# The last row tiles of a decoder trunk by halves of the tokens, with the final products in another place of VectorE's queue

## The chip, the cores and the metric

The kernel runs on one core of one Trainium2 chip. Its time is the device time of one execution in microseconds (us); the median of three executions stands for it. A core has the engines TensorE (PE in the profile; PEld is its loading of weights), VectorE (DVE), ScalarE (ACT) and GpSimd (POOL), each with its own queue of instructions that it works through in order, a SyncE (SP) that issues transfers, and 16 DMA engines that carry them. ScalarE issues transfers too, from its own queue.

## The reference

A trunk of two layers over 512 tokens with 1024 features, in float32. Cut to what matters here:

```python
for i in range(DEPTH):                       # DEPTH = 2
    ...                                      # mixing of tokens, output projection, residual add
    u = jnp.einsum('bsd,df->bsf', rms_norm(x, norm_mlp[i]), w_up[i])
    x = x + jnp.einsum('bsf,fd->bsd', jnp.square(jax.nn.relu(u)), w_down[i])
    gate = jax.nn.sigmoid(jnp.einsum('bsd,de->bse', rms_norm(x, norm_ple[i]), w_ple_gate[i]))
    x = x + gate * jnp.einsum('bsk,kd->bsd', p[i], w_ple_proj[i])
return rms_norm(x, norm_final)               # x * rsqrt(mean(x*x) + eps) * gain
```

The change lies in the last two lines of the last layer: the gate's projection (1024 by 1024), the projection of the embedding `p` (256 by 1024), the residual add, and the final norm, whose sum runs over all 1024 features of a token.

## The kernel before, in words

Features lie on the partitions and tokens along the free dimension: the residual `X` is eight row tiles of 128 features by 512 tokens, `X[0]` to `X[7]`. A weight tile is 128 by 128; four of them are one transfer of 256 KB (`raw`), which ScalarE rounds to `whi` (line 175) and VectorE turns into the rest `wlo` (line 177). Every product of 128 by 128 by N is three matmuls (lines 218 to 220 in `mm3`: high by high, high by low, low by high), so a row tile of the gate is 8 products, 24 matmuls, into the PSUM tile `gate`, and the projection of `p` is 2 products, 6 matmuls, into the PSUM tile `ple`. A row tile m of the last stage so takes 30 matmuls on TensorE, and then the function `gated` on VectorE and ScalarE: `gu` is the gate times the norm of the layer (line 1156, VectorE, reads `gate`), a tanh (line 1157, ScalarE), `gu` times `ple` (line 1158, VectorE) and the add into `X[m]` (line 1159, VectorE). The square `sq` of `X[m]` follows on ScalarE, it is added to `acc`, and ScalarE scales `X[m]` by the gain `gf`.

In the last layer the row tiles 0 to HALF - 1 are made over all 512 tokens at once, the others twice, for the tokens 0 to 255 and then for 256 to 511, with the same weights. HALF is 5, so three row tiles go by halves. When the last row tile of a half is there, the norm of its tokens is closed: `ss` sums `acc` and the last square over the partitions (line 225, TensorE, small matmuls of one column each, their 64 output rows at a time), ten small instructions on VectorE make the inverse root `rT` (lines 1198 and 230 to 239), and `row_of` (line 266, TensorE, two transposes) spreads it as the row `rb` over all partitions in PSUM (`pr`). ScalarE copies `pr` to `Rs` in SBUF (line 1205). Then come the final products `fin`, X times that row, 128 by 256 each (line 1212), in groups of two row tiles, and each group goes out by a transfer of 256 KB (line 1213), in turn from ScalarE's and SyncE's queue. VectorE makes all eight products of the first half from `pr`, and six of the second; GpSimd makes the two of row tiles 6 and 7 of the second half from `Rs`.

The order of the instructions in an engine's queue is fixed before the run: a scheduler orders them by its own simulation of times and by priorities; the code inside `hp_(3000)` has a higher priority. A dependency added by `add_manual_dep` with the class NoSync orders two instructions of an engine and adds no semaphore. On the chip each instruction then waits in its queue for the semaphores that it names, and everything behind it waits with it.

Of the kernel before, what the change touches and what calls it, by code (L numbers as in the profile page):

```python
# [8 lines left out]
F32 = mybir.dt.float32  # L9
# [4 lines left out]
ALU = mybir.AluOpType  # L14
# [25 lines left out]
    ("pkq", 0, 3): 194, ("pov", 0, 0): 349, ("x1p", 0, 0): 385, ("pv", 0, 1): 460, ("pkq", 1, 0): 246,  # L40
    ("psq", 1, 11): 283,
}
HALF = 5
PEND = 4
PEND2 = 3
RB, HIB, LOB, USB = 3, 4, 6, 8
# [41 lines left out]
def trunk(ctx, tc, xT, xK, pT, posr, pos, wfm, wtm, consts, negi, smalls, gfin, out, dbg=None, depth=L):  # L88
# [9 lines left out]
    def mm_tile(name="mm"):  # L98
        return pp.tile([128, 512], F32, tag="mm", name=name, bufs=2)

    def ps_tile(shape, name):
        return pp.tile(shape, F32, tag="pg", name=name, bufs=2)

    def pa_tile(shape, name):
        return pp.tile(shape, F32, tag="pa", name=name, bufs=4)
# [46 lines left out]
    def hp_(n=HPRI):  # L152
        return tc.high_priority(offset=n)
# [43 lines left out]
    @contextmanager  # L197
    def grp(name, i=0):

        n0 = len(nc.cur_bb.bb.instructions)  # L200
        yield
        new = [q for q in nc.cur_bb.bb.instructions[n0:] if q.engine == mybir.EngineType.PE]
        if name == "large":
            large.setdefault(curl[0], []).extend(new)
        else:
            groups.setdefault((name, curl[0], i), []).extend(new)

    def queue_behind():
        for (name, l, i), n in ANCH.items():
# [185 lines left out]
    for l in range(depth):  # L395
# [758 lines left out]
        def gated(m, ts, ps, pq):  # L1154
            u = hp.tile([128, T], F32, tag="ha", name="gu", bufs=2)[:, ts]
            V.tensor_tensor(u, ps, R[:, ts], ALU.mult)
            A.activation(out=u, in_=u, func=ACTF.Tanh, scale=0.5)
            V.scalar_tensor_tensor(u, u, 1.0, pq, ALU.add, ALU.mult)
            V.scalar_tensor_tensor(X[m][:, ts], u, 0.5, X[m][:, ts], ALU.mult, ALU.add)
# [9 lines left out]
        if final:  # L1169

            for m in range(HALF):
                A.activation(out=X[m], in_=X[m], func=ACTF.Copy, scale=gf[:, m:m + 1])
            outs = []
            nw = 10
            w_t = [w_next() for _ in range(nw * (8 - HALF))]
            pq_t = None
            for hf in range(2):
                ts = slice(256 * hf, 256 * hf + 256)
                for m in range(HALF, 8):
                    w_m = w_t[nw * (m - HALF):nw * (m - HALF) + nw]  # L1180
                    ps = pa_tile([128, 256], "gate")
                    mm3(ps, [(h[:, ts], o[:, ts]) for h, o in XG], True, True, w_m[0:8])
                    pq = mm_tile("ple")[:, 0:256]
                    mm3(pq, [(h[:, ts], o[:, ts]) for h, o in pS], True, True, w_m[8:10])
                    gated(m, ts, ps, pq)
                    q = tp.tile([128, T], F32, tag="sq", name="sq", bufs=2)
                    A.activation(out=q[:, ts], in_=X[m][:, ts], func=ACTF.Square)
                    if m < 7:
                        V.tensor_tensor(nrm.acc[:, ts], nrm.acc[:, ts], q[:, ts], ALU.add)
                    A.activation(out=X[m][:, ts], in_=X[m][:, ts], func=ACTF.Copy, scale=gf[:, m:m + 1])  # L1190
                with hp_(3000):
                    ss = ps_tile([128, 2], "ss")
                    for b in range(2):
                        bs = slice(256 * hf + 128 * b, 256 * hf + 128 * b + 128)
                        mm_cols(ss[:, b:b + 1], nrm.acc[:, bs], ones[:, 0:1], True, False)
                        mm_cols(ss[:, b:b + 1], q[:, bs], ones[:, 0:1], False, True)
                    ms = pad(tp, [128, 2], "ms", "ms", 2)
                    V.tensor_scalar(ms, ss, 1.0 / D, EPS, ALU.mult, ALU.add)
                    rT = pad(tp, [128, 2], "rT", "rT", 2)
                    rsqrt(rT, ms, [128, 2], tp, "rn")  # L1200
                    pr = ps_tile([128, 256], "rb")
                    for b in range(2):
                        row_of(pr[:, b * 128:(b + 1) * 128], rT[:, b:b + 1])
                    Rs = hp.tile([128, 256], F32, tag="Rs", name="Rs", bufs=2)
                    A.activation(out=Rs, in_=pr, func=ACTF.Copy)
                outs.append((ts, pr, Rs))
            for ts, pr, Rs in outs:
                for g, ms_g in enumerate(((0, 1), (2, 3), (6, 7), (4, 5))):
                    o_t = hp.tile([128, 256 * len(ms_g)], F32, tag="fin", name="fin", bufs=8)
                    for j, m in enumerate(ms_g):  # L1210
                        e, r_ = (G, Rs) if (g == 2 and ts.start) else (V, pr)
                        e.tensor_tensor(o_t[:, 256 * j:256 * j + 256], X[m][:, ts], r_, ALU.mult)
                    (nc.sync if g % 2 else nc.scalar).dma_start(out=out[ms_g[0]:ms_g[-1] + 1, :, ts].rearrange("m p t -> p m t"),
                                      in_=o_t.rearrange("p (m t) -> p m t", t=256))
        mlp.close()
    queue_behind()

# [129 lines left out]
```

## Time and profile before

| | us |
|---|---|
| median of 3 runs | 1347.64 |
| lowest and highest | 1347.39, 1347.97 |
| profiled execution, its own time | 1348.9 |
| its span, first to last instruction | 1347.1 |
| TensorE busy in the span | 1308.8 |
| VectorE busy | 819.6 |
| ScalarE busy | 606.5 |

The profile is of one execution; the times in its views count from the start of the span. A row of the timeline gives start, duration, engine, line, operation, written tile <- read tiles, shapes, count, and in brackets how long the engine had been idle and which instruction released it. A row of the stretches gives the busy time of each engine in that stretch (with the count), TensorE's granted clock as a share of full speed, the share of the DMA engines and GB/s.

### The profile page before, as it was taken

How to read it: one execution, taken by the hardware profiler on the slowest of the kernel's cores; microseconds unless marked ns; L12 is line 12 of the kernel's file. 1: busy time of each engine (PE TensorE's matmuls, PEld its weight loads, DVE VectorE, ACT ScalarE, POOL GpSimd, SP SyncE). 2: the span in 40 equal slices, each digit the busy share in tenths (PEclk: the TensorE clock that was granted, in tenths of full speed). 3: DMA queues.
4: the chain of work that ended last, by engine and by line, in shares of the span. 5: the costliest groups of instructions: out<-in, count | busy, mean ns of one | idle time of the engine just before them, and what ended most of it. 6: DMA issues, size and time to landing. Idle time of an engine off the chain costs nothing.

```text
span 1347.1 us, 21029 instructions
## 1 busy us (share of the span) xinstructions
PE 1308.8 (97%) x7772; PEld 1081.6 (80%) x7772; DVE 819.6 (61%) x1765; ACT 606.5 (45%) x1245; POOL 133.6 (10%) x151
## 2 busy tenths in 40 slices
PE   9979999999999999999999999999999999999996
PEld 8757787888888888888887877778888888888886
DVE  5967989754443443455768789877534434344565
ACT  6464674543342432444446546635524324234452
POOL 1031330200000000010112223102000000000110
PEclk9969999999999999999999999999999999999998
DMA  7233231333333333333433322223333333333331
GB/s 251 87 98 86 58 111 56 111 93 101 96 97 99 94 96 100 95 101 104 130 109 102 108 68 79 76 74 106 96 94 96 100 94 101 95 95 101 94 103 63
DMA packets 89751, 131.94 MB, mean 98 GB/s; under 512 B 21664, under 2 KB 30368, under 8 KB 89648
## 3 DMA queue, kind: packets, MB, share of 16 engines
q1 hardware_dynamic: 88560, 129.55, 32.1%
q8 instruction: 61, 1.00, 0.3%
q10 hardware_dynamic: 1088, 1.05, 0.2%
q14 instruction: 42, 0.34, 0.1%
HBM read 125.02 MB, written 5.54 MB: 97 GB/s over the span
## 4 chain that ended last, share of the span: by engine, by line
PE 86%; DVE 9%; issue 1%; DMA 1%; ACT 1%; SPq 1%; DVEq 0%; ACTq 0%
PE up L218 9%; PE up L219 9%; PE down L219 9%; PE up L220 9%; PE down L218 9%; PE down L220 9%; PE proj L218 3%; PE proj L219 3%; PE proj L220 3%; PE outp L218 2%; PE gate L218 2%; PE gate L220 2%; PE gate L219 2%; PE outp L219 2%; PE outp L220 2%
## 5 line engine op out<-in xcount | busy, mean ns | idle before, releaser
L175 ACT ACTIVATE whi<-raw 128x512 fp32r<-128x512 f32 x404 | 253.5, 631 | 532.1 <-PE down L219 227.6
L177 DVE TENSOR_TENSOR wlo<-raw,whi 128x512 fp32r<-128x512 f32 x404 | 288.8, 718 | 166.2 <-ACT whi L175 165.1
L218 PE MATMUL down<-hidh,whi 128*128 128x512 f32 x512 | 199.3, 389 | 0.0
L218 PE MATMUL up<-xsh,whi 128*128 128x512 f32 x512 | 199.1, 390 | 0.0
L219 PE MATMUL up<-xsl,whi 128*128 128x512 f32 x512 | 199.0, 389 | 0.0
L220 PE MATMUL up<-xsh,wlo 128*128 128x512 f32 x512 | 199.0, 389 | 0.0
L220 PE MATMUL down<-hidh,wlo 128*128 128x512 f32 x512 | 198.0, 389 | 0.0
L219 PE MATMUL down<-hidl,whi 128*128 128x512 f32 x512 | 198.0, 389 | 0.0
L279 POOL TENSOR_TENSOR acc<-acc,sq 128x512 f32<-128x512 f32 x29 | 40.1, 1381 | 848.9 <-ACT sq L278 848.9
L218 PE MATMUL proj<-xsh,whi 128*128 128x512 f32 x304 | 122.4, 403 | 0.2
L219 PE MATMUL proj<-xsl,whi 128*128 128x512 f32 x304 | 121.3, 399 | 0.0
L220 PE MATMUL proj<-xsh,wlo 128*128 128x512 f32 x304 | 120.9, 398 | 0.0
L1133 DVE TENSOR_TENSOR X<-X,down 128x512 f32<-128x512 f32 x64 | 44.0, 687 | 115.0 <-PE down L220 115.0
L218 PEld LDWEIGHTS down<-hidh,whi 128*128 128x128 f32 x512 | 96.1, 188 | 20.1
L218 PEld LDWEIGHTS up<-xsh,whi 128*128 128x128 f32 x512 | 96.1, 188 | 19.9
L220 PEld LDWEIGHTS up<-xsh,wlo 128*128 128x128 f32 x512 | 96.1, 188 | 19.9
L219 PEld LDWEIGHTS down<-hidl,whi 128*128 128x128 f32 x512 | 96.1, 188 | 19.8
L220 PEld LDWEIGHTS down<-hidh,wlo 128*128 128x128 f32 x512 | 96.1, 188 | 19.9
L219 PEld LDWEIGHTS up<-xsl,whi 128*128 128x128 f32 x512 | 96.1, 188 | 19.8
L1124 DVE SCALAR_TENSOR_TENSOR ha<-up,R 128x512 f32<-128x512 f32 x64 | 44.0, 691 | 91.2 <-PE up L220 88.5
L246 DVE TENSOR_TENSOR hidl<-hf,hidh 128x512 fp32r<-128x512 f32 x64 | 44.3, 692 | 43.9 <-ACT hidh L245 43.9
L218 PEld LDWEIGHTS proj<-xsh,whi 128*128 128x128 f32 x304 | 58.1, 191 | 12.8 <-ACT sqq L581 0.4
(361 smaller groups left out, 2084.2 us busy)
## 6 DMA issues: line engine op xcount, KB each, us to landing
raw<-wfm SPq DMA_DIRECT2D x404, 256.0 KB, 2.6
X<-xT SPq DMA_DIRECT2D x16, 256.0 KB, 4.6
raw<-wtm SPq DMA_DIRECT2D x16, 200.0 KB, 3.9
xk<-xK SPq DMA_DIRECT2D x8, 256.0 KB, 4.6
gr<-scr SPq DMA_DIRECT2D x8, 256.0 KB, 4.1
Mr<-scr SPq DMA_DIRECT2D x8, 256.0 KB, 3.8
xd<-X SPq DMA_DIRECT2D x8, 256.0 KB, 2.3
X<-xd SPq DMA_DIRECT2D x8, 256.0 KB, 3.4
```

What stands on the lines that cost most here:

```text
L175: A.activation(out=hi, in_=raw, func=ACTF.Copy)
L177: (G if (i % NCH) * WC < WPOOL else V).tensor_tensor(lo, raw, f(hi), ALU.subtract)
L218: PE.matmul(out=ps, lhsT=wh, rhs=ah, start=start and k == 0, stop=False)
L219: PE.matmul(out=ps, lhsT=wh, rhs=al, start=False, stop=False)
L220: PE.matmul(out=ps, lhsT=wl, rhs=ah, start=False, stop=stop and k == n - 1)
L246: V.tensor_tensor(lo, src, f(hi), ALU.subtract)
L279: (G if self.n < 6 else V).tensor_tensor(self.acc, self.acc, q, ALU.add)
L1124: V.scalar_tensor_tensor(a_t, ps, 0.0, R, ALU.max, ALU.mult)
L1133: V.tensor_tensor(X[m], X[m], ps, ALU.add)
```

## The change: what it does

Four edits in the last stage, and bookkeeping around them.

1. HALF goes from 5 to 4: row tile 4 is now also made by halves. The stretches of tokens stand in PARTS, (256, 256) as before.
2. The function `last_on` finds the instruction that was last put into VectorE's queue. After each `gated` of a half it notes the add into `X[m]`. Each of the first half's final products is ordered on VectorE behind the noted instruction BEH = -3 of the second half, that is the add into `X[5]` for the tokens 256 to 511.
3. In the first half no `Rs` is made any more (no one read it there). In the second half the row is spread twice: `pr` as before, for VectorE, and `p2` in a PSUM tile of the kind that the gates use, which ScalarE copies to `Rs` for GpSimd.
4. The `fin` tiles are 768 wide and six instead of 512 wide and eight; small tiles of the norm have other names.

```diff
--- before.py
+++ after.py
@@ -40,7 +40,9 @@
     ("pkq", 0, 3): 194, ("pov", 0, 0): 349, ("x1p", 0, 0): 385, ("pv", 0, 1): 460, ("pkq", 1, 0): 246,
     ("psq", 1, 11): 283,
 }
-HALF = 5
+HALF = 4
+PARTS = (256, 256)
+BEH = -3
 PEND = 4
 PEND2 = 3
 RB, HIB, LOB, USB = 3, 4, 6, 8
@@ -204,6 +206,9 @@
             large.setdefault(curl[0], []).extend(new)
         else:
             groups.setdefault((name, curl[0], i), []).extend(new)
+
+    def last_on(engine):
+        return next(q for q in reversed(nc.cur_bb.bb.instructions) if q.engine == engine)
 
     def queue_behind():
         for (name, l, i), n in ANCH.items():
@@ -1173,45 +1178,58 @@
             outs = []
             nw = 10
             w_t = [w_next() for _ in range(nw * (8 - HALF))]
-            pq_t = None
-            for hf in range(2):
-                ts = slice(256 * hf, 256 * hf + 256)
+            t0 = 0
+            for n in PARTS:
+                ts = slice(t0, t0 + n)
+                t0 += n
+                done = []
                 for m in range(HALF, 8):
                     w_m = w_t[nw * (m - HALF):nw * (m - HALF) + nw]
-                    ps = pa_tile([128, 256], "gate")
+                    ps = pa_tile([128, n], "gate")
                     mm3(ps, [(h[:, ts], o[:, ts]) for h, o in XG], True, True, w_m[0:8])
-                    pq = mm_tile("ple")[:, 0:256]
+                    pq = mm_tile("ple")[:, 0:n]
                     mm3(pq, [(h[:, ts], o[:, ts]) for h, o in pS], True, True, w_m[8:10])
                     gated(m, ts, ps, pq)
+                    done.append(last_on(mybir.EngineType.DVE))
                     q = tp.tile([128, T], F32, tag="sq", name="sq", bufs=2)
                     A.activation(out=q[:, ts], in_=X[m][:, ts], func=ACTF.Square)
                     if m < 7:
                         V.tensor_tensor(nrm.acc[:, ts], nrm.acc[:, ts], q[:, ts], ALU.add)
                     A.activation(out=X[m][:, ts], in_=X[m][:, ts], func=ACTF.Copy, scale=gf[:, m:m + 1])
+                nb = n // 128
                 with hp_(3000):
-                    ss = ps_tile([128, 2], "ss")
-                    for b in range(2):
-                        bs = slice(256 * hf + 128 * b, 256 * hf + 128 * b + 128)
+                    ss = ps_tile([128, nb], "ss")
+                    for b in range(nb):
+                        bs = slice(ts.start + 128 * b, ts.start + 128 * b + 128)
                         mm_cols(ss[:, b:b + 1], nrm.acc[:, bs], ones[:, 0:1], True, False)
                         mm_cols(ss[:, b:b + 1], q[:, bs], ones[:, 0:1], False, True)
-                    ms = pad(tp, [128, 2], "ms", "ms", 2)
+                    ms = pad(tp, [128, nb], f"ms{n}", f"ms{n}", 2)
                     V.tensor_scalar(ms, ss, 1.0 / D, EPS, ALU.mult, ALU.add)
-                    rT = pad(tp, [128, 2], "rT", "rT", 2)
-                    rsqrt(rT, ms, [128, 2], tp, "rn")
-                    pr = ps_tile([128, 256], "rb")
-                    for b in range(2):
+                    rT = pad(tp, [128, nb], f"rT{n}", f"rT{n}", 2)
+                    rsqrt(rT, ms, [128, nb], tp, f"rn{n}")
+                    pr = ps_tile([128, n], "rb")
+                    for b in range(nb):
                         row_of(pr[:, b * 128:(b + 1) * 128], rT[:, b:b + 1])
-                    Rs = hp.tile([128, 256], F32, tag="Rs", name="Rs", bufs=2)
-                    A.activation(out=Rs, in_=pr, func=ACTF.Copy)
-                outs.append((ts, pr, Rs))
-            for ts, pr, Rs in outs:
+                    Rs = None
+                    if t0 == T:
+                        p2 = pa_tile([128, n], "rb")
+                        for b in range(nb):
+                            row_of(p2[:, b * 128:(b + 1) * 128], rT[:, b:b + 1])
+                        Rs = hp.tile([128, n], F32, tag="Rs", name="Rs")
+                        A.activation(out=Rs, in_=p2, func=ACTF.Copy)
+                outs.append((ts, n, pr, Rs, done))
+            for k, (ts, n, pr, Rs, _) in enumerate(outs):
                 for g, ms_g in enumerate(((0, 1), (2, 3), (6, 7), (4, 5))):
-                    o_t = hp.tile([128, 256 * len(ms_g)], F32, tag="fin", name="fin", bufs=8)
+                    o_t = hp.tile([128, 768], F32, tag="fin", name="fin", bufs=6)[:, 0:n * len(ms_g)]
                     for j, m in enumerate(ms_g):
-                        e, r_ = (G, Rs) if (g == 2 and ts.start) else (V, pr)
-                        e.tensor_tensor(o_t[:, 256 * j:256 * j + 256], X[m][:, ts], r_, ALU.mult)
+                        e, r_ = (G, Rs) if g == 2 and Rs is not None else (V, pr)
+                        e.tensor_tensor(o_t[:, n * j:n * j + n], X[m][:, ts], r_, ALU.mult)
+                        if Rs is None:
+
+                            tc.add_manual_dep(last_on(mybir.EngineType.DVE), outs[k + 1][4][BEH].name, mybir.DependencyInfo(
+                                mybir.DependencyClass.NoSync, mybir.DependencyReason.DATA), reason="order on VectorE")
                     (nc.sync if g % 2 else nc.scalar).dma_start(out=out[ms_g[0]:ms_g[-1] + 1, :, ts].rearrange("m p t -> p m t"),
-                                      in_=o_t.rearrange("p (m t) -> p m t", t=256))
+                                      in_=o_t.rearrange("p (m t) -> p m t", t=n))
         mlp.close()
     queue_behind()
```

Up to the last row tiles the queues of all engines are the same in both kernels, line numbers aside (a line of `mm3` is 5 higher after the change, and `fin` is L1226 in place of L1212). On VectorE the first half's final products stood in a row before the last row tile's `gu` times `ple`. Before:

```order
L239 SCALAR_TENSOR_TENSOR rT<-rnw,rT 128x2
L1158 SCALAR_TENSOR_TENSOR gu<-gu,ple 128x256
L1159 SCALAR_TENSOR_TENSOR X<-gu,X 128x256
L1189 TENSOR_TENSOR acc<-acc,sq 128x256
L1156 TENSOR_TENSOR gu<-gate,R 128x256
L1212 TENSOR_TENSOR fin<-X,rb 128x256 x8
L1158 SCALAR_TENSOR_TENSOR gu<-gu,ple 128x256
L1159 SCALAR_TENSOR_TENSOR X<-gu,X 128x256
L1198 TENSOR_SCALAR ms<-ss 128x2
L230 TENSOR_SCALAR rnw<-ms 128x2
```

Here `gu<-gate`, `gu<-ple` and `X<-gu,X` are the steps of `gated`, and `ms<-ss` opens the closing of the norm. With the change, in the same place of the queue (the end of the second half):

```order
L1163 SCALAR_TENSOR_TENSOR gu<-gu,ple 128x256
L1164 SCALAR_TENSOR_TENSOR X<-gu,X 128x256
L1197 TENSOR_TENSOR acc<-acc,sq 128x256
L1226 TENSOR_TENSOR fin<-X,rb 128x256 x5
L1161 TENSOR_TENSOR gu<-gate,R 128x256
L1226 TENSOR_TENSOR fin<-X,rb 128x256 x3
L1163 SCALAR_TENSOR_TENSOR gu<-gu,ple 128x256
L1164 SCALAR_TENSOR_TENSOR X<-gu,X 128x256
L1161 TENSOR_TENSOR gu<-gate,R 128x256
L1197 TENSOR_TENSOR acc<-acc,sq 128x256
L1163 SCALAR_TENSOR_TENSOR gu<-gu,ple 128x256
L1164 SCALAR_TENSOR_TENSOR X<-gu,X 128x256
```

The eight products are now around the `gu<-gate` of row tile 6, five ahead of it and three behind; the last row tile's three steps have only an add to `acc` between them.

What each first product of a half waits for is in the rows with their semaphores. Before, for the second half:

```order
L237 TENSOR_TENSOR rnw<-rT 128x2 [waits DVE_49]
L238 SCALAR_TENSOR_TENSOR rnw<-rnw,ms 128x2 [waits DVE_49]
L239 SCALAR_TENSOR_TENSOR rT<-rnw,rT 128x2 [waits DVE_49]
L1212 TENSOR_TENSOR fin<-X,rb 128x256 [waits Activation_49]
L1212 TENSOR_TENSOR fin<-X,rb 128x256 x5
```

and with the change:

```order
L243 SCALAR_TENSOR_TENSOR rn256w<-rn256w,ms_13238 128x2 [waits DVE_49]
L244 SCALAR_TENSOR_TENSOR rT_13240<-rn256w,rT_13240 128x2 [waits DVE_49]
L1226 TENSOR_TENSOR fin<-X,rb 128x256 [waits PE_49]
L1226 TENSOR_TENSOR fin<-X,rb 128x256 x3
L1226 TENSOR_TENSOR fin<-X,rb 128x256 [waits DMAHW4_49]
L1226 TENSOR_TENSOR fin<-X,rb 128x256
```

The first product waited for ScalarE (its copy of `pr`) and now waits for TensorE. The fifth waits for a transfer of the first half, whose `fin` tile it takes.

On TensorE the end of the queue was, before:

```order
L219 MATMUL ple<-pSl,whi 128x256
L220 MATMUL ple<-pSh,wlo 128x256
L225 MATMUL ss<-cst,acc 64x1 x2
L225 MATMUL ss<-cst,sq 64x1 x2
L225 MATMUL ss<-cst,acc 64x1 x2
L225 MATMUL ss<-cst,sq 64x1 x2
L266 MATMUL rb<-cst,rT 128x128 x2
```

and is now:

```order
L224 MATMUL ple<-pSl,whi 128x256
L225 MATMUL ple<-pSh,wlo 128x256
L230 MATMUL ss<-cst,acc 64x1 x2
L230 MATMUL ss<-cst,sq 64x1 x2
L230 MATMUL ss<-cst,acc 64x1 x2
L230 MATMUL ss<-cst,sq 64x1 x2
L271 MATMUL rb<-cst,rT_13240 128x128 x4
```

Behind the two transposes of `pr` stand the two of `p2`.

## Prediction

> **What bounds the kernel now.** I read the page first, then the chain of waits, the stretches and the timeline of the last 45 us, since the queues differ nowhere else.
>
> ```profile
> span 1347.1 us, 21029 instructions
> PE 86%; DVE 9%; issue 1%; DMA 1%; ACT 1%; SPq 1%; DVEq 0%; ACTq 0%
> ```
>
> The chain is TensorE's for most of the span. What this change can move is the piece behind TensorE's last product and the length of TensorE's own work ahead of it. The stretches below are the row tiles of the last stage: row tile 4 over all tokens, row tile 7 of the first half, and row tiles 5, 6 and 7 of the second half.
>
> ```profile
> 1303.51:1310.31 6.80, 6.80 (x32) 5.63 (x31) 5.40 (x9) 6.10 (x11) 2.60 (x2) 1.00 0.47 145
> ...
> 1317.50:1321.10 3.60, 3.60 (x33) 3.60 (x31) 1.69 (x4) 1.34 (x4) 0.00 (x0) 1.00 0.00 0
> 1321.10:1325.10 4.00, 4.00 (x37) 3.85 (x35) 1.27 (x3) 1.34 (x4) 0.00 (x0) 1.00 0.00 0
> 1325.10:1329.33 4.23, 4.23 (x44) 4.08 (x43) 2.88 (x13) 1.34 (x4) 0.00 (x0) 1.00 0.01 4
> 1329.33:1333.14 3.81, 3.81 (x34) 3.76 (x32) 1.95 (x6) 1.73 (x5) 0.00 (x0) 1.00 0.01 2
> ```
>
> TensorE has no idle time in any of them: up to 1333.14 its length sets the end. A half takes 3.60 where nothing is put in, and 4.00, 4.23 and 3.81 where the first half's `ss` and `rb` are. Behind it VectorE and ScalarE set the end:
>
> ```profile
> 1316.98 0.42 DVE L1156 TENSOR_TENSOR gu<-gate,R 128x256 f32<-128x256 f32 x1 [0.78 <-PE gate L220]
> 1318.86 0.42 ACT L1187 ACTIVATE sq<-X 128x256 f32<-128x256 f32 x1 [1.00 <-DVE X L1159]
> 1320.58 0.42 DVE L1156 TENSOR_TENSOR gu<-gate,R 128x256 f32<-128x256 f32 x1 [0.85 <-PE gate L220]
> ...
> 1332.62 0.42 DVE L1156 TENSOR_TENSOR gu<-gate,R 128x256 f32<-128x256 f32 x1 [1.05 <-PE gate L220]
> 1332.96 2.73 DVE L1212 TENSOR_TENSOR fin<-X,rb 128x256 f32<-128x256 f32 x8
> 1335.61 0.41 DVE L1158 SCALAR_TENSOR_TENSOR gu<-gu,ple 128x256 f32<-128x256 f32 x1
> 1336.51 0.42 ACT L1187 ACTIVATE sq<-X 128x256 f32<-128x256 f32 x1 [3.02 <-DVE X L1159]
> ```
>
> Row tile 6 of the first half shows `gated` undisturbed: 1.88 from `gu` to `sq`. The last row tile takes 3.89, because eight `fin` products of the first half, which nobody needs yet, stand in VectorE's queue ahead of its `gu` times `ple`. What follows is serial:
>
> ```profile
> 1336.98 0.38 PE L225 MATMUL ss<-cst,sq 128*64 128x1 f32 x4 [3.47 <-ACT sq L1187]
> ...
> 1337.43 0.36 PE L225 MATMUL ss<-cst,sq 128*64 128x1 f32 x4
> 1337.84 0.16 DVE L1198 TENSOR_SCALAR ms<-ss 128x2 f32<-128x2 f32 x1 [1.36 <-PE ss L225]
> 1339.92 0.66 PE L266 MATMUL rb<-cst,rT 128*128 128x128 f32 x2 [2.13 <-DVE rT L239]
> 1340.61 0.38 ACT L1205 ACTIVATE Rs<-rb 128x256 f32<-128x256 f32 x1 [3.14 <-PE rb L266]
> 1341.03 2.08 DVE L1212 TENSOR_TENSOR fin<-X,rb 128x256 f32<-128x256 f32 x6 [1.26 <-ACT Rs L1205]
> 1341.07 1.41 POOL L1212 TENSOR_TENSOR fin<-X,Rs 128x256 f32<-128x256 f32 x2 [26.92 <-ACT Rs L1205]
> 1341.81 1.13 ACTq L1213 DMA_DIRECT2D outT<-fin  x2
> ```
>
> VectorE's last products read `pr` in PSUM, yet wait for ScalarE's copy of it, 0.42 after the row was there.
>
> **The change part by part.**
>
> *Row tile 4 by halves.* It takes 2 x 3.60 = 7.20 in place of 6.80. The second half then has four row tiles, with `ss` and `rb` in the first three of them, so the last one is free of them. Its start on TensorE is 1303.51 + 4 x 3.60 + 4.00 + 4.23 + 3.81 = 1329.95, and its `gu` comes 3.08 later (1317.50 to 1320.58 in the first half): 1333.03, against 1332.62. Cost: +0.41.
>
> The Trainium skill ("TensorE: Matmul & The Clock Gate", Back-to-back issue gap) gives N / 2.4 + 2.5 ns between warm matmuls; an estimate by it is 30 x 216 = 6.47 for the whole row tile and 60 x 109 = 6.55 for two halves, a cost of 0.08 and a sum 0.3 lower. The trace disagrees: 3.60 / 30 is 120 ns for N = 256, with the loading of weights busy all the time, and 6.80 / 30 is 227 for N = 512.
>
> *The eight products out of the last row tile.* Undisturbed, its `sq` comes 1.88 after `gu`: 1333.03 + 1.88 = 1334.91. Before it took 3.89. Gain: -2.01. The products go to row tile 6 of the second half, whose `gu` can start at 1303.51 + 14.40 + 4.00 + 4.23 + (1332.62 - 1329.33) = 1329.43. They wait for the first half's `rb`, which stands 21 products into that row tile:
>
> ```profile
> 1325.67 0.28 PE L225 MATMUL ss<-cst,sq 128*64 128x1 f32 x4
> ...
> 1325.92 0.26 PE L225 MATMUL ss<-cst,sq 128*64 128x1 f32 x4
> ...
> 1331.85 0.38 PE L266 MATMUL rb<-cst,rT 128*128 128x128 f32 x2
> ...
> 1332.27 0.39 ACT L1205 ACTIVATE Rs<-rb 128x256 f32<-128x256 f32 x1 [0.61 <-PE rb L266]
> ```
>
> Before, the row could be read 0.35 ahead of that row tile's `gu` (1332.27 against 1332.62), so the products start at 1329.08. One takes 0.331 (1332.96 to 1335.61 for eight). Five end at 1330.74, `gu` of row tile 6 goes then, 1.31 late, the other three end at about 1332.07, and `gu` times `ple` and the add follow by about 1332.87. Behind them in the queue is the last row tile's `gu`, due at 1333.03: 0.16 of slack, so I cost the delay at nothing. The cover is TensorE's work on the last row tile; if each product took its whole 0.42 instead, that `gu` would be 8 x 0.09 - 0.16 = 0.55 late. Two transfers now stand in ScalarE's queue around row tile 6's tanh; the first is free with the second product, at about 1329.8, before that tanh is due at 1331.2, and the second behind it, before `sq`: nothing.
>
> *The row twice.* VectorE need not wait for ScalarE: it starts where `Rs` started before. Gain: 1341.03 - 1340.61 = 0.42, taken as -0.41 since its wait ends about 0.01 after the row. The price is on GpSimd's path: two more transposes stand ahead of `Rs`. The bounds for the pair are 0.2 (a warm pair of transposes lengthens a half by 3.81 - 3.60) and 0.66 (the cold row's whole duration). GpSimd ended its products 1.87 after `Rs` started (1342.48), so it would end 2.07 to 2.53 after VectorE's start, where VectorE's own six end at 2.08. Does the last transfer mind?
>
> ```profile
> DMA  0000000000000005999999999999999200000000
> GB/s 0 0 0 0 0 0 0 0 0 0 0 0 0 0 0 185 387 392 335 346 387 381 387 387 381 392 381 370 387 392 358 64 0 0 0 0 0 0 0 0
> ```
>
> These are 40 slices of 1340.00 to 1347.10, 0.1775 each. Once the second half's transfers run (from 1342.66, 0.85 after the first issue), the DMA engines are full until all four are through, 2.75 for 1.05 MB, 0.69 each. The third transfer's turn comes 0.78 + 0.85 + 2 x 0.69 = 3.0 after VectorE's first product; GpSimd's is ready 2.07 + 0.85 = 2.9 to 3.4 after it, and SyncE's last one, ready at 2.9, fills a hole. So the end follows VectorE's first product: cost 0, at most 0.25 if half the hole stays.
>
> *TensorE's clock behind its last product.*
>
> ```profile
> 1335.75:1336.00 0.25, 0.00 (x0) 0.00 (x0) 0.25 (x1) 0.00 (x0) 0.00 (x0) 0.83 1.10 393
> 1336.00:1336.25 0.25, 0.00 (x0) 0.00 (x0) 0.21 (x2) 0.00 (x0) 0.00 (x0) 0.50 1.09 377
> ```
>
> The granted clock fell to half at about 1335.92, 2.4 after TensorE went idle (1336.98 - 3.47 = 1333.51). Cold, the last twelve matmuls of `ss` took 0.81 (1336.98 to 1337.79); warm, in the first half, 0.51 (1325.67 to 1326.18). After the change TensorE goes idle at about 1334.0 (1333.03, six `ple` matmuls and the first of `ss`) and the squares' `ss` comes at 1334.91 + 0.47 = 1335.4, 1.4 later, which is sooner than the fall was: I take it warm, -0.30; the other bound is 0. The row: from the transposes to where it can be read 0.69 cold (1339.92 to 1340.61) and 0.42 warm (1331.85 to 1332.27), so 0 to -0.27. It comes some 4 after TensorE first went idle, later than the fall: I take 0.
>
> The Trainium skill (same page, Part 1) has the clock halve after a window of idleness of about 3.4 us, windows that run freely, so that the moment differs between runs. This trace fits (2.4 can be the end of a window that was partly busy), but one run can't show the freedom.
>
> *The rest.*
>
> ```profile
> outT<-fin SPq DMA_DIRECT2D x4, 256.0 KB, 2.2
> ```
>
> Six wider `fin` tiles: the fifth product of VectorE waits for a transfer issued some 8 us earlier, against 2.2 that such a transfer takes: nothing. GpSimd's add of row tile 4 to `acc` moves to VectorE as two halves, in the idle time that the stretches show: nothing.
>
> **Sum:** +0.41 - 2.01 - 0.41 - 0.30 = -2.31, on the profiled span of 1347.1 (own time 1348.9, 1.3 above the median). The three unprofiled times differ by 0.58, about the 0.57 of the two clock terms, so the median may hold part of them already; I take -2.2 from the median 1347.64: 1345.4.
>
> **Rivals.**
>
> 1. *The clock stays full to the end.* Then the row's 0.27 comes on top: -2.6, 1345.0. For it: TensorE's pause ahead of `ss` shrinks from 3.5 to about 1.4. Against: behind `ss` comes another of 2.1.
>
> 2. *The products arrive late, or GpSimd's half ends last.* With 0.55 of delay to the last `gu`, 0.25 at the end and a cold `ss` the sum is -2.31 + 0.30 + 0.55 + 0.25 = -1.2, 1346.4. For it: the slack is only 0.16, and worked out from rows of another place. Against: the pitch of 0.331 held over fourteen products.
>
> 3. *The tie buys nothing*, 1347.6: the time at the end is set by something other than VectorE's products, say the transfers. Against: 3.89 against 1.88 is in the rows, and VectorE's queue now has the products elsewhere.
>
> 4. *Slower: weights.* In the first half TensorE now goes through the weights of row tiles 4 to 7 in 14.4 instead of 6.80 + 10.79, so those of row tile 7 are wanted 3.2 sooner. If they come later than that, TensorE stands still, and each us late is a us on the end.
>
> ```profile
> 1306.54 0.33 SPq L171 DMA_DIRECT2D raw<-wfm  x1
> ...
> 1309.94 0.69 DVE L177 TENSOR_TENSOR wlo<-raw,whi 128x512 fp32r<-128x512 f32 x1
> ```
>
> The last weights were ready at 1310.6. They are wanted for row tile 7 from about 1303.51 + 3 x 3.60 = 1314.3 on: TensorE would stop from 3.7 of lateness on, the kernel would be slower from 3.7 + 2.3 = 6.0, and 8.8, a little more than a row tile's 6.80, makes 1347.64 - 2.3 + 5.1 = 1350.4. Against: the new `gu` and tanh of row tile 4, which now stand ahead of the last weights, wait for TensorE only until 1303.51 + 3.08 = 1306.6, before those weights were made. For it: the rows show the weights' pace under the old demand only.
>
> **How the numbers follow.** The forecast has 0.63, rival 1 has 0.14, rival 2 has 0.12, rival 3 has 0.06 and rival 4, at its last price, has 0.05. Changes within 0.2% (2.7 us, about what a measurement of this kernel can tell from no change) count as the same, so faster means below 1344.94. Half of rival 1 and a seventh of the forecast (noise of 0.3) lie there: 0.16. Slower is rival 4: 0.05. The same is the rest, 0.79. The forecast's own range is 1345.0 to 1345.9. The range of 8 in 10 takes in rivals 1 and 2, 1344.7 to 1346.6.
>
> **What would show it.** Right: no `fin` between the last row tile's `gu` and its `gu` times `ple`, and 1.9 from its `gu` to its `sq`; its `gu` at 1333.0; the twelve `ss` in 0.5; VectorE's last products released by TensorE and not by ScalarE, at about 1338.7; transfers without a hole. Wrong: the last row tile's `gu` released by VectorE's own work instead of by `gate`; an idle TensorE between 1303 and 1333; a clock already at half at `ss`; a hole in the DMA row of the end ahead of GpSimd's group.

## The result, and the profile after

| | before | change |
|---|---|---|
| median of 6 runs, us | 1347.81 | 1361.41 |
| ratio to before | | 1.0091, 95% interval 1.0072 to 1.0109 |
| profiled execution: own time | 1348.9 | 1361.63 |
| its span | 1347.1 | 1359.8 |

Single executions at a lower granted clock (one of the change, 1457.08, and one in the runs below, 2416.0 of the kernel before with the spare tile of 128 bytes) are in the medians, but not in the ratios.

The forecast was 1345.4 within 1344.7 to 1346.6. The change made the kernel 0.9% slower. The page after, its span, its busy times and its chain:

```profile
span 1359.8 us, 21099 instructions
...
PE 1323.2 (97%) x7804; PEld 1083.4 (80%) x7804; DVE 821.5 (60%) x1770; ACT 606.6 (45%) x1247; POOL 131.4 (10%) x150
...
PE 86%; DVE 9%; issue 2%; ACT 1%; DMA 1%; POOL 0%; SPq 0%; POOLq 0%; DVEq 0%; ACTq 0%
```

TensorE is busy for 1323.2 in place of 1308.8, and no other engine differs by as much as 3. 32 more matmuls do not make 14.4 us. To see where it lies, one instruction that stands in both kernels well ahead of the changed code serves as a mark: ScalarE's copy of the last layer's norm row, `R`, which every row tile of the last stage needs. Its row in the timeline, before and after:

```profile
1291.43 0.60 ACT L302 ACTIVATE R<-rb 128x512 f32<-128x512 f32 x1 [1.39 <-PE rb L266]
```

```profile
1306.09 0.60 ACT L307 ACTIVATE R<-rb 128x512 f32<-128x512 f32 x1 [1.42 <-PE rb L271]
```

It comes 14.66 later, and nothing of the changed code has run by then. From there to the end it was 1347.1 - 1291.43 = 55.67 before and is 1359.8 - 1306.09 = 53.71 now: the part that the change is about became 1.96 shorter. The loss is in the part that it does not touch. A stretch of the first layer, where TensorE goes through products of 128 by 128 by 512 without idle time, before and after (the columns are those of the stretches in the prediction):

```profile
300.00:400.00 100.00, 100.00 (x443) 82.83 (x442) 43.65 (x66) 36.31 (x58) 0.00 (x0) 1.00 0.33 98
```

```profile
300.00:400.00 100.00, 100.00 (x437) 81.73 (x437) 42.55 (x64) 35.30 (x56) 0.00 (x0) 1.00 0.32 95
```

The granted clock is 1.00 in both, TensorE never stops, and yet it gets through 437 matmuls in place of 443. The groups of the page say which ones. Before (busy time, mean ns of one):

```profile
L218 PE MATMUL down<-hidh,whi 128*128 128x512 f32 x512 | 199.3, 389 | 0.0
L218 PE MATMUL up<-xsh,whi 128*128 128x512 f32 x512 | 199.1, 390 | 0.0
```

After:

```profile
L223 PE MATMUL down<-hidh,whi 128*128 128x512 f32 x512 | 202.2, 395 | 0.0
L225 PE MATMUL down<-hidh,wlo 128*128 128x512 f32 x512 | 201.0, 395 | 0.0
...
L223 PE MATMUL up<-xsh,whi 128*128 128x512 f32 x512 | 199.0, 390 | 0.0
```

The product into `down` takes 6 ns longer, the product into `up`, of the same shape and the same number, does not. The weight loads of both (PEld) take 188 ns each, before and after. Matmuls overlap, so the distance between the starts of neighbours, the pitch, says what one costs. Worked out from the starts in the trace, from each matmul into `down` to the next one where that goes into `down` too, its mean is 226.7 ns before and 233.3 after, for `up` 227.0 and 227.1. With 1536 matmuls of `down` that is 1536 x 6.6 = 10.1 us; another 552 matmuls of that width read tiles that lie near those of `down` and are slower too: 288 of `gate` by 5.5 ns, 192 of the output projection by 3.4 and 72 of `ple` by 4.9, together 2.6 us. The sum is about 13 of the 14.66; the rest is of the size by which the stages ahead vary between executions (before took 1346.1 to 1352.2 in the runs below).

The two have the same shapes and the same queue as before; one thing that the change does to `down` and not to `up` is to move an operand in memory. In the program as built, edit 4's new names (`ms256`, `rT256`, `rn256w`) make six more tiles of 64 bytes per partition, since the old names stay in use in the other norms. They stand in a pool ahead of the one that holds `hid` (the moved operand of `down` and of the gate), and everything behind them lies 6 x 64 = 384 bytes further on: the first `hid` tile starts at byte 101504 in place of 101120, that is 128 past a multiple of 256 in place of at one. The weights `whi` and `wlo`, and `xs`, the moved operand of `up`, did not move.

The last row tile and what follows, from the timeline after:

```profile
1343.92 1.75 DVE L1226 TENSOR_TENSOR fin<-X,rb 128x256 f32<-128x256 f32 x5 [0.65 <-PE rb L271]
...
1345.58 0.42 DVE L1161 TENSOR_TENSOR gu<-gate,R 128x256 f32<-128x256 f32 x1
1345.92 1.07 DVE L1226 TENSOR_TENSOR fin<-X,rb 128x256 f32<-128x256 f32 x3
...
1347.84 0.42 DVE L1161 TENSOR_TENSOR gu<-gate,R 128x256 f32<-128x256 f32 x1
...
1349.66 0.42 ACT L1195 ACTIVATE sq<-X 128x256 f32<-128x256 f32 x1 [0.55 <-DVE X L1164]
...
1350.13 0.28 PE L230 MATMUL ss<-cst,sq 128*64 128x1 f32 x4 [1.01 <-ACT sq L1195]
...
1350.69 0.16 DVE L1207 TENSOR_SCALAR ms<-ss 128x2 f32<-128x2 f32 x1 [1.06 <-PE ss L230]
...
1353.47 2.08 DVE L1226 TENSOR_TENSOR fin<-X,rb 128x256 f32<-128x256 f32 x6 [0.84 <-PE rb L271]
```

No `fin` stands in the last row tile any more, and it takes 1349.66 - 1347.84 = 1.82 from `gu` to `sq`, against 3.89 before. VectorE's last products are released by TensorE. So the forecast of the last stage can be followed on its own.

### The profile page after: what moved, and what is told of

Same layout as the page of the kernel before. It is cut to its first block, busy times and chain, and to the rows that moved or that the text cites. A ratio compares the mean times of both kernels' runs of the same rounds, so it can differ in the third digit from the quotient of the medians.

```text
span 1359.8 us, 21099 instructions
## 1 busy us (share of the span) xinstructions
PE 1323.2 (97%) x7804; PEld 1083.4 (80%) x7804; DVE 821.5 (60%) x1770; ACT 606.6 (45%) x1247; POOL 131.4 (10%) x150
## 4 chain that ended last, share of the span: by engine, by line
PE 86%; DVE 9%; issue 2%; ACT 1%; DMA 1%; POOL 0%; SPq 0%; POOLq 0%; DVEq 0%; ACTq 0%
PE down L225 9%; PE down L224 9%; PE down L223 9%; PE up L223 9%; PE up L224 9%; PE up L225 9%; PE proj L223 3%; PE proj L224 3%; PE proj L225 3%; PE outp L223 2%; PE gate L223 2%; PE gate L224 2%; PE gate L225 2%; PE outp L224 2%; PE outp L225 2%
## 5 line engine op out<-in xcount | busy, mean ns | idle before, releaser
L223 PE MATMUL down<-hidh,whi 128*128 128x512 f32 x512 | 202.2, 395 | 0.0
L225 PE MATMUL down<-hidh,wlo 128*128 128x512 f32 x512 | 201.0, 395 | 0.0
L224 PE MATMUL down<-hidl,whi 128*128 128x512 f32 x512 | 200.9, 395 | 0.0
```

The source lines that it names most:

```text
L223: PE.matmul(out=ps, lhsT=wh, rhs=ah, start=start and k == 0, stop=False)
L224: PE.matmul(out=ps, lhsT=wh, rhs=al, start=False, stop=False)
L225: PE.matmul(out=ps, lhsT=wl, rhs=ah, start=False, stop=stop and k == n - 1)
```

## The experiments

The theory, A in the texts on record, is that the place of the operands in memory sets the pitch of the matmuls. The rivals are that something else of the change slows the matmuls (its other tiles, its order of instructions), or that the names do it in another way than by moving tiles.

### 1. Names against the rest

The change with the old names, so that no tile is added; its queues are those of the change:

```diff
-                    ms = pad(tp, [128, nb], f"ms{n}", f"ms{n}", 2)
+                    ms = pad(tp, [128, nb], "ms", "ms", 2)
-                    rT = pad(tp, [128, nb], f"rT{n}", f"rT{n}", 2)
-                    rsqrt(rT, ms, [128, nb], tp, f"rn{n}")
+                    rT = pad(tp, [128, nb], "rT", "rT", 2)
+                    rsqrt(rT, ms, [128, nb], tp, "rn")
```

> The change whole, but the norm's small tiles of the last stage keep their old names (ms, rT, rn), so that they share the tiles of the other norms, as before. The queues of all engines are those of the change. Theory A (addresses): the three new names put six tiles of 64 bytes, 384 bytes together, ahead of the tiles that the `down`, `gate`, `ple` and half of the `outp` matmuls read; those tiles then start 128 bytes past a multiple of 256, and each of these matmuls takes 2 to 5% longer. Without the names `down` is back at 227 ns a matmul, and what is left is the work on the tail: 1347.7 - 2.3 = 1345.4, range 1344.8 to 1346.2. Theory B (the edits of the last stage cost the time, by the order, the extra matmuls or the longer program): still 1358 to 1362.

The kernel before with only the three new names:

```diff
-                    ms = pad(tp, [128, 2], "ms", "ms", 2)
+                    ms = pad(tp, [128, 2], "ms256", "ms256", 2)
-                    rT = pad(tp, [128, 2], "rT", "rT", 2)
-                    rsqrt(rT, ms, [128, 2], tp, "rn")
+                    rT = pad(tp, [128, 2], "rT256", "rT256", 2)
+                    rsqrt(rT, ms, [128, 2], tp, "rn256")
```

> The kernel before, with nothing but the three new names for the small tiles of the last norm (so 384 bytes more ahead of the tiles of the mixing and the MLP). The queues are those of the kernel before. Theory A: the whole loss and none of the gain, 1347.7 + 14.5 = 1362, `down` at 230 to 238 ns a matmul. Theory B: no difference, 1347.7.

The change with its new names, and a tile of 128 bytes more ahead of them, which makes the shift 512 bytes:

```diff
+    spare = tp.tile([128, 32], F32, tag="spare", name="spare", bufs=1)
+    V.memset(spare, 0.0)
```

> The change whole, new names and all, with one more tile of 128 bytes ahead, so that the tiles of the mixing and the MLP lie 512 bytes further than in the kernel before: at a multiple of 256 again. One more small memset at the start. Theory A, if the multiple of 256 decides: as with the old names, 1345.4, `down` at 227 ns. Theory C (any move of these tiles costs, or the names themselves do): 1360 as with the change.

And the kernel before with that spare tile alone, old names, a shift of 128 bytes:

> The kernel before with one tile of 128 bytes ahead of those of the mixing and the MLP, which then start 128 past a multiple of 256, as with the change, but by 128 instead of 384 bytes. Theory A: slower by about 14, 1362. Theory C (the distance of 384 matters, a border that some tile crosses): near 1347.7. Theory B: 1347.7.

Measured: the change with old names 1346.57 against 1348.87 for before on the same chip, ratio 0.9984 (0.9970 to 0.9997); before with new names 1364.35, ratio 1.0107 (1.0084 to 1.0130); the change with new names and the spare tile 1348.16, ratio 0.9986 (0.9973 to 1.0000); before with the spare tile 1362.90, ratio 1.0095 (1.0069 to 1.0121). The groups of the page in the first three:

```profile
L223 PE MATMUL down<-hidh,whi 128*128 128x512 f32 x512 | 199.2, 389 | 0.0
```

```profile
L218 PE MATMUL down<-hidh,whi 128*128 128x512 f32 x512 | 202.2, 395 | 0.0
```

```profile
L226 PE MATMUL down<-hidh,whi 128*128 128x512 f32 x512 | 199.2, 389 | 0.0
```

What follows: the names alone cost the whole loss, and the rest of the change makes the kernel faster. It is not the names as such, since with a spare tile beside them they cost nothing, and a spare tile under the old names costs the same as they do. It is the shift.

### 2. How far a shift counts

The kernel before with a spare tile of 64, and of 256 bytes:

```diff
+    spare_tp = tp.tile([128, 16], F32, tag="spare", name="spare_tp", bufs=1)
+    V.memset(spare_tp, 0.0)
```

> The kernel before with 64 bytes more ahead of the tiles of the mixing and the MLP, which then start 64 past a multiple of 256. The runs so far showed 227 ns a `down` matmul at a multiple of 256 and 230 or 238, 233 in the mean, at 128 past one. Theory A1 (every start off a multiple of 256 costs, as the row of 2048 bytes then reaches into nine stretches of 256 instead of eight): again 233 in the mean and about 1362. Theory A2 (128 past is the bad place, by an odd and even of something): 227 and 1348, or a value of its own.

> The kernel before with 256 bytes more, so that the tiles of the mixing and the MLP start at a multiple of 512; in all runs with 227 ns a matmul so far they started at an odd multiple of 256. If 256 is what counts: no difference, 1348, `down` at 227. If the rows like a multiple of 512: `down` faster than 227, and up to 14 us off. If only odd multiples of 256 are good: slower.

Measured, against 1348.25 for before beside them: 64 bytes 1354.94, ratio 1.0049 (1.0031 to 1.0066); 256 bytes 1348.46, ratio 1.0003 (0.9990 to 1.0016). At 64 bytes the three matmuls of a product differ:

```profile
L221 PE MATMUL down<-hidh,whi 128*128 128x512 f32 x512 | 201.7, 394 | 0.0
L223 PE MATMUL down<-hidh,wlo 128*128 128x512 f32 x512 | 199.4, 392 | 0.0
...
L222 PE MATMUL down<-hidl,whi 128*128 128x512 f32 x512 | 197.5, 388 | 0.0
```

The mean pitch of `down` is 229.0 at 64 bytes and 226.7 at 256. So 256 bytes count as none, and the price isn't one of all or nothing: at 64 bytes it is (229.0 - 226.7) / 6.6, about a third, by the pitch, and about half by the ratios (1.0049 against 1.0095 at 128 bytes). Of the outcomes that the text on record had named, the full price (1362) was a miss; it came out as the "value of its own".

### 3. Which operand

Spare tiles ahead of the weights, of `xs` and of the pool `tp` move each class on its own. The weights 128 bytes off, all moved operands at multiples of 256 (the weight tiles of the last row tiles lie in the pool of `xs`: they stay at a multiple of 256 here, and are moved with `xs` in the next kernel):

```diff
+    spare_wp = wp.tile([128, 32], F32, tag="spare", name="spare_wp", bufs=1)
+    V.memset(spare_wp, 0.0)
+    spare_xs = xs.tile([128, 96], F32, tag="spare", name="spare_xs", bufs=1)
+    V.memset(spare_xs, 0.0)
```

> The kernel before with 128 bytes ahead of the weights' tiles (`raw`, `whi`, `wlo`) and 384 behind them: the weights start 128 past a multiple of 256, everything else at one, as before. If the start counts for the moved operand alone (the 512 columns that stream): 1348, all matmuls at 227. If it counts for the loaded weights too: `up`, `down`, `gate` and `proj` are all slower, by up to 6 ns times some 5000 matmuls of this width, 1348 + 30.

`xs` 128 bytes off, the weights of `up` and `down` and `hid` at multiples of 256:

```diff
+    spare_xs = xs.tile([128, 32], F32, tag="spare", name="spare_xs", bufs=1)
+    V.memset(spare_xs, 0.0)
+    spare_tp = tp.tile([128, 96], F32, tag="spare", name="spare_tp", bufs=1)
+    V.memset(spare_tp, 0.0)
```

> The kernel before with 128 bytes ahead of the tiles `xs` that hold the moved operand of `up` and `proj` (and half of that of `outp`), and 384 behind them: these start 128 past a multiple of 256, those of `down` and `gate` at one. Theory A predicts the loss in the other place: `up` and `proj` at 233, `down` and `gate` at 227, and 6.6 ns times (1536 + 912 + 192) = 17 us: 1365. If the loss hangs on something special to the tiles of `down` and `gate` (their writers, their number): 1348.

Everything 128 bytes off, weights and moved operands alike, by the first of the two lines of `spare_wp` and its memset alone:

> The kernel before with 128 bytes ahead of the weights' tiles and nothing else, so that weights and moved operands all start 128 past a multiple of 256, at the same distance from each other as in the kernel before. Theory A-absolute (each operand's own start counts): `up`, `down`, `gate` and `proj` at 233 or more, the two losses of before perhaps added, 1372 to 1395. Theory A-relative (the two operands are read at the same time and only their distance to each other counts): all at 227, 1348.

Measured: weights moved 1373.73, ratio 1.0192 (1.0171 to 1.0212), where 1348 was expected if the moved operand counted by itself and 1348 + 30 if the loaded weights count too: it is the second, at a somewhat lower price. `xs` moved 1361.94, ratio 1.0104 (1.0084 to 1.0124), where theory A said 1365: the loss is in the other place, as it said, and a little smaller. Each of these two kernels ran twice. All moved 1347.92 against 1350.46, ratio 0.9993 (0.9975 to 1.0011). The groups with the weights moved:

```profile
L223 PE MATMUL down<-hidh,whi 128*128 128x512 f32 x512 | 202.0, 395 | 0.0
L223 PE MATMUL up<-xsh,whi 128*128 128x512 f32 x512 | 201.8, 395 | 0.0
```

With `xs` moved:

```profile
L223 PE MATMUL up<-xsh,whi 128*128 128x512 f32 x512 | 202.0, 396 | 0.0
...
L223 PE MATMUL down<-hidh,whi 128*128 128x512 f32 x512 | 199.3, 389 | 0.0
```

With all moved:

```profile
L221 PE MATMUL down<-hidh,whi 128*128 128x512 f32 x512 | 199.2, 389 | 0.0
L221 PE MATMUL up<-xsh,whi 128*128 128x512 f32 x512 | 198.9, 390 | 0.0
```

Whichever of the two is moved, the matmuls of 512 columns that pair a moved tile with an unmoved one are slow; move both, and none is. The starts (bytes past a multiple of 256) are those of the built programs, the pitches means of the trace's starts in ns:

| kernel | weights | `xs` | `hid` | pitch `down` | pitch `up` | ratio |
|---|---|---|---|---|---|---|
| before | 0 | 0 | 0 | 226.7 | 227.0 | 1 |
| change | 0 | 0 | 128 | 233.3 | 227.1 | 1.0091 |
| before, 64 bytes | 0 | 0 | 64 | 229.0 | 227.2 | 1.0049 |
| before, 256 bytes | 0 | 0 | 0 | 226.7 | 227.0 | 1.0003 |
| weights moved | 128 | 0 | 0 | 232.4 | 232.7 | 1.0192 |
| `xs` moved | 0 | 128 | 0 | 226.8 | 233.3 | 1.0104 |
| all moved | 128 | 128 | 128 | 226.7 | 227.0 | 0.9993 |

What counts is the distance between the start of the weights that are loaded and the start of the operand that is moved, modulo 256 bytes, and not where either of them starts. The runs have the distances 0, 64 and 128 and no others; shifts of 256, 384 and 512 did as 0, 128 and 0. Why the distance counts, no run here shows.

### 4. The parts of the last stage

With the old names, so that nothing is shifted, the two steps of the forecast were taken out one at a time, in one execution each. HALF back at 5 with all else kept:

```diff
-HALF = 4
+HALF = 5
```

> The change with the old names and HALF = 5: row tile 4 over all tokens again, three row tiles by halves; the tie and the second row stay. In VectorE's queue the first half's products then stand around the last row tile's `gu` (five ahead of it, three behind), since the first half's row comes in the last row tile again. The figure is the time from the start of `R` (the layer's last norm row) to the end of the span: 55.7 in the kernel before, 53.2 with the change and the old names. If row tile 4 by halves is what makes room for the products, as the sum has it (cost 0.41, gain 2.0): 55.7 - 0.4 (row twice) - 0.4 (five products start earlier) = 54.9. If the tie does it: 52.8.

And one row in place of two:

```diff
-                        p2 = pa_tile([128, n], "rb")
-                        for b in range(nb):
-                            row_of(p2[:, b * 128:(b + 1) * 128], rT[:, b:b + 1])
-                        A.activation(out=Rs, in_=p2, func=ACTF.Copy)
+                        A.activation(out=Rs, in_=pr, func=ACTF.Copy)
```

> The change with the old names, but the last row is spread once, and ScalarE copies it from there, as before: the two extra transposes go, VectorE's last products wait for ScalarE's copy again. Time from the start of `R` to the end: 53.2 with the second row. By the sum 0.4 more: 53.6. If the second row's transposes on TensorE and the later `Rs` cost as much as the wait saves: 53.2.

The stages ahead vary by some us between executions (before took 1344.6 to 1351.56 beside these two), so tenths are read from `R` to the end of the span. The rows of HALF = 5:

```profile
1290.87 0.60 ACT L307 ACTIVATE R<-rb 128x512 f32<-128x512 f32 x1 [1.39 <-PE rb L271]
```

```profile
1331.70 1.74 DVE L1226 TENSOR_TENSOR fin<-X,rb 128x256 f32<-128x256 f32 x5 [0.70 <-PE rb L271]
1333.36 0.41 DVE L1161 TENSOR_TENSOR gu<-gate,R 128x256 f32<-128x256 f32 x1
1333.70 1.07 DVE L1226 TENSOR_TENSOR fin<-X,rb 128x256 f32<-128x256 f32 x3
...
1336.06 0.28 PE L230 MATMUL ss<-cst,sq 128*64 128x1 f32 x4 [3.12 <-ACT sq L1195]
...
1336.62 0.16 DVE L1207 TENSOR_SCALAR ms<-ss 128x2 f32<-128x2 f32 x1 [1.07 <-PE ss L230]
```

Its span is 1345.5, so `R` to the end is 54.6, as expected if the gain hangs on HALF (54.9), and not 52.8. The eight products are back around the last row tile's `gu`, although the tie is in the code: it is the smaller HALF that moves them, because the first half's row then comes one row tile earlier. The tie of edit 2 is worth nothing in this kernel: with HALF = 4 and no tie the scheduler makes the same queues, word for word.

With one row, `R` starts at 1293.69 and the span is 1347.4, 53.7 to the end, against 53.2 with two (53.6 was expected). VectorE waits for ScalarE's copy again:

```profile
1340.20 0.66 PE L271 MATMUL rb<-cst,rT 128*128 128x128 f32 x2 [2.13 <-DVE rT L244]
...
1341.31 2.07 DVE L1223 TENSOR_TENSOR fin<-X,rb 128x256 f32<-128x256 f32 x6 [1.26 <-ACT Rs L1216]
```

From the start of the row to the products it takes 1.11, against 0.65 with two rows (below): 0.46 for the second row.

## Why the prediction was wrong, point by point

**The step that failed** is the premise of the prediction's first paragraph, which looks at the last 45 us alone "since the queues differ nowhere else". With it goes the paragraph on the rest: it costs the wider `fin` tiles and the moved add, but not the names of the front part's "small tiles of the norm have other names", which were never costed. They are no instruction, so a count of instructions and queues does not show them. What they do is to shift all tiles behind them by 384 bytes, and the runs put some 15 us on that: 1364.35 against 1348.87 for the names alone, and 1361.41 against 1346.57 for the change with and without them. The statement that the queues differ nowhere but in the last 45 us was right; the conclusion that the time could differ nowhere else was not. The profile of before could not have shown this price, as the operands of all its matmuls of 512 columns start at multiples of 256 there. The shift itself could have been read from the starts of the tiles in the built program. The Trainium skill ("SBUF — State Buffer", Operand start alignment) asks that an operand starts at a multiple of its element size, and speaks of what is legal. Every kernel here keeps to that (all shifts are multiples of 64 bytes), and the section puts no price on a start. The rows above put 6.6 ns on each matmul of `down`.

**The sum for the last stage** can be set against the change with the old names. Its rows of the end:

```profile
1289.71 0.60 ACT L307 ACTIVATE R<-rb 128x512 f32<-128x512 f32 x1 [1.39 <-PE rb L271]
```

```profile
1327.34 1.74 DVE L1226 TENSOR_TENSOR fin<-X,rb 128x256 f32<-128x256 f32 x5 [0.69 <-PE rb L271]
1329.00 0.41 DVE L1161 TENSOR_TENSOR gu<-gate,R 128x256 f32<-128x256 f32 x1
```

```profile
1330.77 0.42 DVE L1164 SCALAR_TENSOR_TENSOR X<-gu,X 128x256 f32<-128x256 f32 x1
...
1331.28 0.42 DVE L1161 TENSOR_TENSOR gu<-gate,R 128x256 f32<-128x256 f32 x1
...
1333.10 0.42 ACT L1195 ACTIVATE sq<-X 128x256 f32<-128x256 f32 x1 [0.55 <-DVE X L1164]
...
1333.57 0.28 PE L230 MATMUL ss<-cst,sq 128*64 128x1 f32 x4 [1.04 <-ACT sq L1195]
...
1334.13 0.16 DVE L1207 TENSOR_SCALAR ms<-ss 128x2 f32<-128x2 f32 x1 [1.06 <-PE ss L230]
...
1336.21 1.04 PE L271 MATMUL rb<-cst,rT 128*128 128x128 f32 x4 [2.13 <-DVE rT L244]
1336.86 2.08 DVE L1226 TENSOR_TENSOR fin<-X,rb 128x256 f32<-128x256 f32 x6 [0.80 <-PE rb L271]
...
1337.75 1.41 POOL L1226 TENSOR_TENSOR fin<-X,Rs 128x256 f32<-128x256 f32 x2 [29.34 <-ACT Rs L1219]
```

In us from the start of `R` (the forecast's times less 1291.43):

| | forecast | change, old names | change |
|---|---|---|---|
| first half's products start | 37.65 | 37.63 | 37.83 |
| `gu` of row tile 6 | 39.31 | 39.29 | 39.49 |
| last `gu` | 41.60 | 41.57 | 41.75 |
| last `sq` | 43.48 | 43.39 | 43.57 |
| `ss` of the last square | 43.97 | 43.86 | 44.04 |
| VectorE's last products | 47.27 | 47.15 | 47.38 |
| end of the span | 53.36 | 53.19 | 53.71 |

- *Row tile 4 by halves, +0.41*: the last `gu` is at 41.57, before at 1332.62 - 1291.43 = 41.19: +0.38.
- *Eight products out of the last row tile, -2.01*: `gu` to `sq` takes 1.82, against 3.89: -2.07. Taken out with HALF = 5, this term and the one before it were worth 54.6 - 53.2 = 1.4 together, and not 1.6: there VectorE starts the products ahead of the `gu` and its last `sq` comes at 44.7 after `R`, against 45.1 in the kernel before.
- *The slack of 0.16*: VectorE ends the add into `X` at 1330.77 + 0.42 = 1331.19 and takes `gu` at 1331.28. About 0.1 was left. The prediction named a `gu` that isn't released by `gate` as a sign of error; the row has no releaser, and still it was not late.
- *The row twice, -0.41*: 0.46 from the row's start to the products, 0.5 from `R` to the end. GpSimd ends at 1337.75 + 1.41 = 1339.16, 2.3 after VectorE's start, within the 2.07 to 2.53 given.
- *The clock, -0.30*: the last twelve matmuls of `ss` took from 1333.57 to the `ms` at 1334.13, as long as warm ones, at a granted clock of 1.00 against 0.50 before. But so they did with HALF = 5 (from 1336.06 to 1336.62, at 1.00) behind a pause of 3.12, near the 3.47 of before, where they were cold. So the term came as forecast, but it isn't shown that it is due to the shorter pause.
- *The transfers*: from VectorE's last products to the end of the span 1342.9 - 1336.86 = 6.04, before 6.07: the end does follow the products.

The whole is 53.19 - 55.67 = -2.48 against -2.31, and on the median 1346.57 against 1348.87, -2.3. The mechanism of the change was sized well, and with the old names it is the faster of the two kernels, by 0.16% (0.03% to 0.30%).

**The rivals.** Rival 1, a full clock to the end, was given -2.6; the change with the spare tile comes to that. There the granted clock stays full until about 1335.5, past the middle of the row's four transposes:

```profile
1335.14 0.72 PE L274 MATMUL rb<-cst,rT 128*128 128x128 f32 x4 [2.13 <-DVE rT L247]
...
1335.58 2.07 DVE L1229 TENSOR_TENSOR fin<-X,rb 128x256 f32<-128x256 f32 x6 [0.59 <-PE rb L274]
```

With the same pause of 2.13 ahead of it the row took 0.72 there and 1.04 with the old names, where the clock fell at about 1336.3, just behind the row's start; and from `R` (1288.63) to the end it was 1341.7 - 1288.63 = 53.07, -2.6. The Trainium skill ("TensorE: Matmul & The Clock Gate", Part 1) has windows that run freely, so that the moment of the fall differs between runs. These two rows agree with it, as do the pauses of 3.12 and 3.47 above. Rival 2 had a last `gu` 0.55 late and 0.25 lost at the end: the `gu` was on time, and GpSimd did end last, 0.2 behind VectorE (1336.86 + 2.08), but at no price to the end. Rival 3, no gain at all, is refuted by the 53.19. Rival 4 is on the right side for the wrong reason: TensorE is busy for all of the 30.12 us of that stage's halves (the last row shown below). The kernel became slower by something that no rival named, and the 0.05 for slower covered only what could be read from the queues.

## What to carry to other kernels

A change of names, of a buffer's width or of a small tile can move every address behind it: compare the starts of the large operands, modulo 256 bytes, before counting instructions. Where TensorE bounds a kernel with matmuls of 512 float32 columns, keep weights and moved operands at the same remainder of 256 bytes; a spare tile does it. When a small edit costs more than everything in it, look for one operation whose mean moved in a stage that was not touched.

## What the runs showed that was not expected

The pitch of a float32 matmul of 128 by 128 by 512, with a weight load for each, was 227 ns where the weights and the moved operand start at the same remainder of 256 bytes, 229 where they are 64 apart and 232 to 233 where they are 128 apart, by runs with either of them moved. Those of 400 columns (the products into `tok`) pay less: 181.5 ns where both start alike, 184.3 with the weights moved and 184.4 with `xs` moved, 181.5 again with all moved. Those of 256 columns did not mind: the 259 matmuls of the last stage that go by halves, nearly all 256 wide and from the same shifted tiles, took as long in the change as with the old names:

```profile
1318.43:1348.50 30.07, 30.07 (x259) 29.57 (x257) 20.43 (x54) 14.17 (x31) 2.59 (x2) 1.00 0.19 64
```

```profile
1301.78:1331.90 30.12, 30.12 (x259) 29.68 (x257) 20.62 (x54) 14.60 (x31) 2.59 (x2) 1.00 0.21 67
```

The transfers out have a smaller price of their own. From VectorE's last products to the end of the span it took 6.04 to 6.12 in the eight kernels whose `fin` tiles start at a multiple of 256 bytes, and 6.33 to 6.39 in the five where they start 64 or 128 past one. All moved by 128 is among the latter (6.34), with matmuls at full pace, so this is another matter than the matmuls. The Trainium skill ("DMA: Bandwidth & Descriptors", How a descriptor splits into AXI transactions) has the first transaction of a piece that does not start at a multiple of 256 bytes begin at the boundary below its start, so that bytes are fetched that are not used. The 0.27 us between the two groups agree with it in direction, though no run here counts transactions.
